# The output projection of a two-layer hybrid trunk computed as seven block products instead of eight

## The chip, the core and the metric

The kernel runs on one core of a Trainium2 chip. The metric is the device time of one execution in microseconds (us). All weights come from device memory during the execution, and all data is float32.

## What is computed

One trunk of two layers works on a sequence of 512 tokens, 1024 wide. What matters here is the middle of each layer:

```python
g_a, g_m = jnp.split(gates, 2, axis=-1)
mixed = jax.nn.sigmoid(g_a) * (att @ w_att_branch) + jax.nn.sigmoid(g_m) * (hm @ w_m_branch)
x = x + mixed @ w_out                       # 512x1024 @ 1024x1024

u = jax.nn.relu(rmsnorm(x, norm_ffn) @ w_ff1)   # 1024 -> 4096
x = x + (u * u) @ w_ff2                         # 4096 -> 1024
```

Ahead of it stand a normalisation, one large input projection, a windowed attention that gives `att`, and a matrix-memory branch that gives `hm` (both 512 wide). The text calls the second of them the m branch.

## The kernel before

**Precision by three products.** `mm3` (L182) makes every large product of three matmuls: each operand is cut into a high and a low part in a format that TensorE takes, and high x high, high x low and low x high are summed in PSUM. A cut takes one copy on ScalarE (the high part) and one subtraction on VectorE (the low part). Weights are cut by `chunk` (L139: one 128x512 tile at a time, copy L165, subtraction L166), activations by `split` (L171: L175 to L179). In the MLP `two_parts` (L866) cuts 128x1024 at a time (copy L867, subtraction L868).

**Groups of four banks.** Outside the MLP a projection is a list of steps from `group_steps` (L188): a group takes four PSUM banks (the pool `psum` holds five of them under the tag `m`, and `paux` three more), runs over the rows k of the weights with four 128-wide tiles m in the inner loop, and evacuates its four banks in `finish` once the last k is done. `feat_steps` (weights stationary, features on the partitions) and `tok_steps` (activations stationary, tokens on the partitions) build on it. `weave` (L222) places side work between the steps at positions counted in units of 12 matmuls.

**The end of the mixer** (L810 to L841) is the place of the change:

- Two groups for the m branch (L823 to L830), each with four k and four m, so 16 steps and 48 matmuls. `ev_m` multiplies the bank by the gate (L826), adds the attention branch's product (L827) and cuts the sum (`split`, L828).
- Two groups for the output projection (L834 to L840), each with eight k and four token blocks: 96 matmuls of 128x512. `ev_x` adds the four banks onto the residual stream `xtok` (L837). Four sets of four transposes for the next normalisation (`norm.steps`, L277) are woven into the second of them.

**The MLP** (L843 on) already uses seven block products in place of eight for its two matrix products: `first_slots` (L1008) and `second_slots` (L1167), with sums of weight blocks made by transfers that add to what lies in memory (`more`, L1025 and L1182, issued from GpSimd's queue) and with VectorE sums. There the products of the two matrices alternate, and each bank pair (`x`, `y`, `f`) rests for at least one product before it is used again. The first four loads of the MLP (`First.load`, L926) go to the buffers r0 to r3 of the pool `raws`.

**Who sets the order.** The kernel is written with Tile, a layer that gets the whole list of instructions with priorities, orders each engine's queue at compile time and places the waits; each engine then runs its queue strictly in order. `tc.high_priority()` puts what it encloses ahead of the rest. A buffer is given to a new tile once its old tile has been read for the last time, also across pools that share an address. SyncE (SP) issues the plain loads, GpSimd (POOL) the adding ones.

**Where pools lie.** The mixer holds, one after another, `wraw` 3 x 2 KB per partition, `wsp` 8 x 2 KB, `act` 32 x 2 KB, `tmp` 17 x 2 KB and `mid`. The MLP takes the same range over with `uraw`, `comb`, `uspl`, `spl` (8 x 4 KB) and `raws` (11 x 4 KB), in this order.

Of the kernel before, what the change touches and what calls it, by code (L numbers as in the profile page):

```python
# [16 lines left out]
P = 128  # L17
# [9 lines left out]
ROPE = 16  # L27
C_Q, C_K, C_V, C_QM, C_VM, C_OM, C_IF, C_G = 0, 512, 640, 768, 1280, 1792, 2304, 2312
NEG = -1.0e30
LN_EXP = "natural_log_exp_and_others"  # L30


@with_exitstack
def hybrid_kernel(ctx, tc, x, norm_mix, w_in, att_q_norm, att_k_norm, att_sinks, m_gate_bias,
# [27 lines left out]
    def nm(s):  # L62
        uid[0] += 1
        return f"{s}_{uid[0]}"
# [1 line left out]

    now = {}

    def pool(phase, name, bufs):
        now[name] = phase.enter_context(tc.tile_pool(name=name, bufs=bufs, reuse_waits="tile"))  # L70
# [137 lines left out]
    def feat_steps(acts, srcs, evac):  # L208

        def mm(ps, c, w, a, first, last):  # L210
            mm3(ps, w[0][:, c], w[1][:, c], a[0], a[1], first, last)

        return group_steps(acts, srcs, evac, T, mm)

    def tok_steps(acts, srcs, evac, width=T, order=None):

        def mm(ps, c, w, a, first, last):
            mm3(ps[:, :width], a[0][:, c], a[1][:, c], w[0][:, :width], w[1][:, :width], first, last)

        return group_steps(acts, srcs, evac, width, mm, order)  # L220

    def weave(fill, side=()):  # L222

        side = sorted(side, key=lambda e: e[0])
        at = 0.0
        for width, f in fill:
            while side and side[0][0] <= at + 1e-6:
                side.pop(0)[1]()
            f()
            at += width  # L230
        for _, f in side:
            f()

    def rsqrt(dst, v, tag):

        shape = list(v.shape)
        t = sm(shape, tag + "t")
        sc.activation(t, v, AF.Ln)
        sc.activation(dst, t, AF.Exp, scale=-0.5)
        t2 = sm(shape, tag + "u")  # L240
# [144 lines left out]
    nc.gpsimd.dma_start(grow[16:24, :], m_head_norm.rearrange("l (k p) -> (l k) p", p=P))  # L385
    wait_x.close()

    def mixer(l, norm, late, order, phase):

        W = w_in[l]  # L390
        pool(phase, "wraw", 3)
        pool(phase, "wsp", 4)
        pool(phase, "act", 32)
        pool(phase, "tmp", 17)
        mid = pool(phase, "mid", 1)

        def wcols(c0, n):
            return lambda k: [W[k * P:(k + 1) * P, c0:c0 + n]]
# [130 lines left out]
        def rope(xv, b, nh):  # L529

            r0 = 0 if nh == HQ else 8
            ct, st = tabs[nh != HQ]
            ve.tensor_tensor(xv, xv, rqk[:, b, r0:r0 + nh].unsqueeze(2).to_broadcast([P, nh, HD]), op=ALU.mult)
            t1 = sm([P, nh, ROPE], f"rp{nh}")
            t2 = sm([P, nh, ROPE], f"rq{nh}")
# [153 lines left out]
        def back(i):  # L689

            with tc.issue_after(i.ins):
                sc.preload_act_table_set(LN_EXP)

        def gate_steps(g, then=lambda: None):
            sg = []

            def ev(m, ps):
                sg.append(slot())
                ve.tensor_tensor(sg[m], ps, row[0], op=ALU.mult)  # L699
# [83 lines left out]
        prod = []  # L783

        def a_steps(g, sg):
            def ev_a(m, ps):
                t = sg[m]
                prod.append(t)
                ve.tensor_tensor(t, t, ps, op=ALU.mult)
# [22 lines left out]
        def head_tr(f):  # L812
            ps = aux()
            for b in range(NB):
# [6 lines left out]
        sgm = [g2, g3]  # L821
        mixed = [None] * KT
        for g in range(2):  # L823
            def ev_m(m, ps, g=g):
                i = 4 * g + m
                ve.tensor_tensor(sgm[g][m], sgm[g][m], ps, op=ALU.mult)  # L826
                ve.tensor_tensor(prod[i], prod[i], sgm[g][m], op=ALU.add)  # L827
                mixed[i] = split(prod[i])  # L828

            weave(feat_steps(hmT, lambda k, g=g: [w_m_branch[l, k * P:(k + 1) * P, 512 * g:512 * g + 512]], ev_m))  # L830


        norm = Norm(lambda k: g_ffn(l, k))
        for j in range(2):  # L834
            def ev_x(b, ps, j=j):
                xb = xtok[b // 2][j][:, b % 2, :]
                ve.tensor_tensor(xb, xb, ps, op=ALU.add)  # L837

            weave(tok_steps(mixed, lambda k, j=j: [w_out[l, k * P:(k + 1) * P, T * j:T * (j + 1)]], ev_x),
                  norm.steps(0, 1.5, 0.5) if j else [])  # L840
        return norm  # L841

    def mlp(l, norm, late, phase):  # L843
# [2 lines left out]


        final = l == DEPTH - 1
        quads = pool(phase, "uraw", 1)
        comb = pool(phase, "comb", 1)  # L850
        uspl = pool(phase, "uspl", 2)
        spl = pool(phase, "spl", 4)
        raws, idle_raws = pool(phase, "raws", 1), list(range(11))
        acts, ms = norm.acts, []
        H = 2 * P

# [405 lines left out]


        us = [{key: quads.tile([P, 4, H], F32, tag=t, name=nm("u")) for key, t in buf[0].items()}, {}, {}, {}]
        f01 = [First(0, "f"), First(1, "y")]
# [6 lines left out]
        slots = [first_slot(2, us[0], "x"), first_slot(3, us[0], "f")]  # L1272
        for part in range(4):
            p = second_slots(part, us[part])
            if part < 3:
# [34 lines left out]
    def turn_behind(norm, k):  # L1310

        with tc.issue_after(latest[0].ins):
            norm.turn(k)
# [4 lines left out]
            + [(3.0 + 2.2 * j, lambda j=j: norm.squares(j)) for j in range(2)])  # L1318
    order = None
    for l in range(DEPTH):  # L1320
        with start if l == 0 else ExitStack() as phase:
            if l > 0:
                psum_pools(phase, 3)
            norm = mixer(l, norm, late, order, phase)
        late = norm.steps(1, 1.5, 0.5)
        with ExitStack() as phase:
            psum_pools(phase, 2)
            norm = mlp(l, norm, late, phase)
        late = norm.steps(0, 1.5, 0.5, lambda k, norm=norm: turn_behind(norm, k)) if norm else []
        order = [4, 5, 6, 7, 0, 1, 2, 3]  # L1330

# [39 lines left out]
```

## Time and profile before

| What | Value |
|---|---|
| Time, median of 3 runs (lowest to highest) | 1303.55 us (1303.52 to 1304.15) |
| Span of the profiled execution, first to last instruction | 1302.9 us |
| The profiled execution's own time | not listed apart from these three; the median is 0.65 us above the span |
| TensorE matmuls / busy share of the span | 6978 / 99% |
| VectorE, ScalarE, GpSimd busy share | 73%, 59%, 15% |
| Output projection, layer 0 (first to last matmul) | 288.6 to 334.0 us |
| Output projection, layer 1 | from 933.8 us |

A span is what the trace covers. A busy share is an average over all stages. "Granted clock" is the share of its full clock that TensorE got; it is 1.00 for the whole execution. In the timeline, PE is TensorE's matmul queue, PEld its weight loads, DVE is VectorE, ACT is ScalarE; a row gives the start, the length of the run of like instructions, the engine, the line, output and inputs with shapes, and in brackets how long the engine had been idle and who ended that.

### The profile page before, as it was taken

Reading aid. Unit: us, or ns where it says so; the run is one execution under the profiler, and the core shown is the slowest. Engines: PE = TensorE matmul, PEld = TensorE weight load, DVE = VectorE, ACT = ScalarE, POOL = GpSimd, SP = SyncE. Lnnn points to the kernel's source line nnn. Section 1 sums busy time; section 2 is a strip of 40 time slices with the busy share of each in tenths; the row PEclk is TensorE's granted clock in tenths of the full one; section 3 lists DMA queues with packets and bytes.
Section 4 is the critical chain, followed back from the end, with each engine's and each line's share of the span. In section 5 each row is a group of like instructions: output and inputs, shape, how many; then the busy total and the mean of one; then the engine's idle time right before and its main releaser. Section 6 shows DMA issues by size and latency. Waiting matters only on the chain. (4 is left out here: it accounts for less than half of the span.)

```text
span 1302.9 us, 19074 instructions
## 1 busy us (share of the span) xinstructions
PE 1291.5 (99%) x6978; PEld 1105.2 (85%) x6978; DVE 955.5 (73%) x1505; ACT 763.7 (59%) x1329; POOL 200.4 (15%) x281
## 2 busy tenths in 40 slices
PE   9999999999999999999999999999999999999998
PEld 6877788888889999999888778888888899999987
DVE  4699754475677897968948996545737878879797
ACT  5578755544466665656555787554445556665563
POOL 4511100000003021131115111000000030311210
PEclk9999999999999999999999999999999999999999
DMA  5422222372369888898124222223714597988953
GB/s 154 110 72 59 74 81 74 90 249 82 98 155 172 236 185 207 195 211 216 33 75 114 65 66 75 79 75 92 256 57 129 141 215 195 201 212 196 213 148 98
DMA packets 130542, 177.61 MB, mean 136 GB/s; under 512 B 9864, under 2 KB 78320, under 8 KB 130448
## 3 DMA queue, kind: packets, MB, share of 16 engines
q1 hardware_dynamic: 94208, 131.82, 32.7%
q0 software_dynamic: 35520, 44.17, 21.2%
q8 instruction: 55, 0.90, 0.3%
q10 hardware_dynamic: 720, 0.40, 0.1%
q14 instruction: 39, 0.32, 0.1%
HBM read 174.27 MB, written 2.10 MB: 135 GB/s over the span
## 5 line engine op out<-in xcount | busy, mean ns | idle before, releaser
L47 PE MATMUL mm<-i,wh 128*128 128x512 f32 (+1 forms) x1280 | 352.7, 362 | 0.0
L867 ACT ACTIVATE wh<-raw 128x1024 fp32r<-128x1024 f32 x212 | 223.1, 1056 | 181.1 <-PE mm L47 114.0
L868 DVE TENSOR_TENSOR wl<-raw,wh 128x1024 fp32r<-128x1024 f32 x212 | 255.2, 1218 | 74.2 <-ACT wh L867 72.3
L47 PEld LDWEIGHTS mm<-i,wh 128*128 128x128 f32 x1280 | 224.3, 189 | 32.1 <-DVE a L699 0.8
L166 DVE TENSOR_TENSOR wl<-w,wh 128x512 fp32r<-128x512 f32 (+1 forms) x208 | 140.8, 679 | 137.7 <-ACT wh L165 129.4
L47 PE MATMUL mm<-i,wl 128*128 128x512 f32 (+1 forms) x640 | 229.8, 360 | 0.0
L165 ACT ACTIVATE wh<-w 128x512 fp32r<-128x512 f32 (+1 forms) x208 | 127.0, 611 | 146.7 <-PE mm L47 122.8
L47 PE MATMUL mm<-wh,uh 128*128 128x512 f32 x440 | 171.8, 390 | 0.0
L47 PE MATMUL mm<-wl,uh 128*128 128x512 f32 x440 | 171.7, 390 | 0.0
L47 PE MATMUL mm<-wh,ul 128*128 128x512 f32 x440 | 171.2, 389 | 0.0
L1027 POOL DMA_DIRECT2D raw<-in_w_ff_dram x48 | 62.3, 1304 | 591.3 <-DMA raw<-in_w_ff_dram 316.9
L47 PE MATMUL mm<-wh,i 128*128 128x512 f32 (+1 forms) x512 | 150.6, 370 | 1.2 <-ACT wh L165 0.6
L47 PEld LDWEIGHTS mm<-i,wl 128*128 128x128 f32 x640 | 120.8, 189 | 18.1 <-DVE wl L868 0.4
L47 PEld LDWEIGHTS mm<-wh,i 128*128 128x128 f32 x512 | 92.0, 188 | 19.0 <-DVE i L179 2.1
L913 DVE SCALAR_TENSOR_TENSOR x<-mm,ms,x 128x512 f32<-128x512 f32 x126 | 90.4, 743 | 9.9 <-PE mm L47 9.9
L47 PEld LDWEIGHTS mm<-wh,ul 128*128 128x128 f32 x440 | 82.6, 188 | 17.4
L47 PEld LDWEIGHTS mm<-wh,uh 128*128 128x128 f32 x440 | 82.8, 188 | 16.1
L47 PEld LDWEIGHTS mm<-wl,uh 128*128 128x128 f32 x440 | 82.8, 188 | 15.6
L47 PE MATMUL mm<-wl,i 128*128 128x512 f32 (+1 forms) x256 | 93.0, 363 | 0.0
L47 PE MATMUL mm<-wh,a 128*128 128x512 f32 x256 | 81.3, 392 | 0.0
L47 PE MATMUL mm<-a,wh 128*128 128x512 f32 x256 | 80.5, 397 | 0.0
L47 PE MATMUL aux<-i,wh 128*128 128x256 f32 x384 | 69.5, 283 | 0.0
(259 smaller groups left out, 2161.0 us busy)
## 6 DMA issues: line engine op xcount, KB each, us to landing
raw<-in_w_ff_dram SPq DMA_DIRECT2D x144, 512.0 KB, 5.2
raw<-in_w_ff_dram POOLq DMA_DIRECT2D x84, 512.0 KB, 7.8
w<-in_w_in_dram SPq DMA_DIRECT2D x128, 256.0 KB, 2.6
w<-in_w_out_dram SPq DMA_DIRECT2D x32, 256.0 KB, 2.7
w<-in_w_att_branch_dram SPq DMA_DIRECT2D x16, 256.0 KB, 2.6
w<-in_w_m_branch_dram SPq DMA_DIRECT2D x16, 256.0 KB, 2.7
w<-in_w_in_dram SPq DMA_DIRECT2D x16, 128.0 KB, 2.1
out_dram<-x SPq DMA_DIRECT2D x7, 256.0 KB, 2.0
```

What stands on the lines that cost most here:

```text
L47: latest[0] = nc.tensor.matmul(*args, **kw)
L165: sc.activation(wh[:, :off], raw[:, :off], AF.Copy)
L166: ve.tensor_tensor(wl[:, :off], raw[:, :off], f32(wh[:, :off]), op=ALU.subtract)
L867: sc.activation(hi, src, AF.Copy)
L868: ve.tensor_tensor(lo, src, f32(hi), op=ALU.subtract)
L913: ve.scalar_tensor_tensor(xh[:, cc], ps[i][:, cc], ms[j][:, b:b + 1], xh[:, cc], op0=ALU.mult, op1=ALU.add)
L1027: gp.dma_start(to[h], src(h, i, j), accum_op=ALU.add)
```

## The change

Four things are changed:

1. The two groups of the output projection become seven block products (24 matmuls each). `mixed` is taken as 2x2 blocks A(t,i), t a half of the tokens and i a half of the features, and `w_out` as 2x2 blocks B(i,j). The operands that are sums of A blocks (`s1` to `s4`) are made by VectorE and GpSimd (`combine`, `later`); the sums of B blocks by transfers that add one block onto another in memory (`more`).
2. The second half of the m branch runs with the tile m in the outer loop and k in the inner one, from two 128x1024 weight tiles that were cut ahead (`prep_m`), so that its four banks end one after another.
3. The PSUM pools of the MLP (three pairs `x`, `y`, `f` and two single banks) are opened ahead of the output projection and kept through the MLP.
4. In memory: the gated attention products move from eight `act` slots into two wide tiles (`prods`, 2 x 8 KB), `act` shrinks from 32 to 25 slots, `tmp` and `mid` move to the far end of the memory and are closed ahead of the output projection, where `wide_raw` (6 x 4 KB) and `wide_split` (8 x 4 KB) take their place; the MLP's `spl` and `raws` come first in its range. Four small tags get two buffers instead of three.

The core of the diff (the pools, the small tags and the attention products are left out):

```diff
+        parts_.close()
+        wide_raw, wide_split = pool(parts_, "wide_raw", 1, "right"), pool(parts_, "wide_split", 4, "right")
+        sgm, H = [g2, g3], 2 * P
...
+        def load(r, w, i, j, h):
+            with tc.high_priority():
+                nc.sync.dma_start(r, block(w, i, j, h))
+        def more(r, i, j, h):
+            with tc.high_priority():
+                gp.dma_start(r, block(w_out, i, j, h), accum_op=ALU.add)
...
+        def wide_parts(r):
+            with tc.high_priority():
+                h, lo = (wide_split.tile([P, 2, T], F32R, tag=t, name=nm(t)) for t in ("vh", "vl"))
+                sc.activation(h, r, AF.Copy)
+                ve.tensor_tensor(lo, r, f32(h), op=ALU.subtract)
+            return h, lo
+        def part(t, i, k):
+            return wide[i][:, 2 * k:2 * k + 2, H * t:H * (t + 1)]
+        def merge(g, m, ps):
+            ve.tensor_tensor(sgm[g][m], sgm[g][m], ps, op=ALU.mult)
+            ve.tensor_tensor(wide[g][:, m, :], wide[g][:, m, :], sgm[g][m], op=ALU.add)
...
+        weave(feat_steps(hmT, lambda k: [w_m_branch[l, k * P:(k + 1) * P, 0:T]], ev_m),
+              [(0.5, lambda: prep_m(0)), (1.0, lambda: prep_m(1))])
...
+        weights = {1: w1, 5: w5, 3: w3, 6: w6, 7: w7, 2: w2, 4: w4}
+        order = (1, 5, 3, 6, 7, 2, 4)
...
+        prepare(2)
+        for h in range(2):
+            with tc.high_priority():
+                u["00", h] = halves(part(0, 0, h))
+        def combine(k):
+            with tc.high_priority():
+                u1, u2, u4 = pair(), pair(), pair()
+                gp.tensor_tensor(u4, part(0, 0, k), part(0, 1, k), op=ALU.subtract)
+                ve.tensor_tensor(u1, part(1, 1, k), part(1, 0, k), op=ALU.subtract)
+                gp.tensor_tensor(u4, u4, u1, op=ALU.add)
+                u["s1", k] = halves(u1)
+                u["s4", k] = halves(u4)
+                ve.scalar_tensor_tensor(u2, u1, -1.0, part(0, 0, k), op0=ALU.mult, op1=ALU.subtract)
+                u["s2", k] = halves(u2)
+        for m in range(4):
+            ps = bank()
+            for k in range(4):
+                c = slice(m * P, (m + 1) * P)
+                hi, lo = wm[k // 2]
+                mm3(ps, hi[:, k % 2, c], lo[:, k % 2, c], hmT[k][0], hmT[k][1], k == 0, k == 3)
+            with tc.high_priority():
+                merge(1, m, ps)
+            if m % 2:
+                combine(m // 2)
+        small_banks.close()
+        psum_pools(wide_banks, 2)
+        def later(k):
+            u3 = pair()
+            gp.tensor_tensor(u3, part(0, 0, k), part(1, 0, k), op=ALU.subtract)
+            u["s3", k] = halves(u3)
+            for t in range(2):
+                u[f"{t}1", k] = halves(part(t, 1, k))
...
+        def onto(t, j, ps, op=ALU.add):
+            with tc.high_priority():
+                ve.tensor_tensor(xtok[t][j], xtok[t][j], ps, op=op)
+        plan = {1: ("x", "00", [(0, 1, ALU.add)]), 5: ("y", "s1", [(1, 0, ALU.subtract)]),
+                3: ("y", "s4", [(0, 0, ALU.subtract)]), 6: ("x", "s2", [(0, 0, ALU.subtract)]),
+                7: ("x", "s3", [(1, 0, ALU.subtract), (1, 1, ALU.add)]), 2: ("f", "01", [(0, 1, ALU.add)]),
+                4: ("y", "11", [(1, 1, ALU.add)])}
+        fresh = (1, 5, 2, 4)
...
+        weave([(0.125, lambda n=n, h=h, step=step: run(n, h, step))
+               for n in order for h in range(2) for step in range(4)],
+              norm.steps(0, 5.5, 0.25))
```

In `plan` the numbers are the names of the products; each has a bank pair, an operand and the quarters (t,j) of the residual stream onto which `onto` adds the pair when the product is done. A product has two halves h; each half takes one cut weight tile of 128x1024 (`prepare` cuts it three to four halves ahead, into one of four buffers) and runs four steps of three matmuls of 128x512. Products that are not in `fresh` add to what is in their pair: 3 goes on in `y` after 5, and 6 and 7 go on in `x` after 1. The additions in place are: onto the tile of product 1 the block for 5, then those for 6 and for 4; onto the tile of product 3 the block for 7. `later` runs behind product 1, without high priority.

More of the change, by code (lines that the diff above doesn't have):

```diff
@@ L386, in hybrid_kernel, with mixer @@
     wait_x.close()
-    def mixer(l, norm, late, order, phase):
+    def mixer(l, norm, late, order, phase, small_banks, wide_banks):
         W = w_in[l]
@@ L692, in back @@
                 sc.preload_act_table_set(LN_EXP)
+        wide = [prods.tile([P, 4, T], F32, tag=f"p{g}", name=nm("p")) for g in range(2)]
         def gate_steps(g, then=lambda: None):
@@ L697, in ev @@
             def ev(m, ps):
-                sg.append(slot())
+                sg.append(wide[g][:, m, :] if g < 2 else slot())
                 ve.tensor_tensor(sg[m], ps, row[0], op=ALU.mult)
@@ L833, in mixer @@
-        norm = Norm(lambda k: g_ffn(l, k))
[L834 to L840, printed above, removed]
+        parts_.close()
+        parts_ = ExitStack()
+        pool(parts_, "edge", 1, "right").tile([P, EDGE], F32, name=nm("edge"))
@@ new lines, in pair, with halves, ev_m, prep_m @@
+        def pair(dt=F32):
+            return slot(dt, (P, 2, H))
+        def halves(src):
+            return split(src, get=lambda: pair(F32R))
+        u = {}
+        def merge(g, m, ps):
+            ve.tensor_tensor(sgm[g][m], sgm[g][m], ps, op=ALU.mult)
+            ve.tensor_tensor(wide[g][:, m, :], wide[g][:, m, :], sgm[g][m], op=ALU.add)
+        def ev_m(m, ps):
+            merge(0, m, ps)
+        def prep_m(h):
+            r = raw(f"c{h}")
+            load(r, w_m_branch, 0, 1, h)
+            wm.append(wide_parts(r))
@@ new lines, in w6, with w7, w2, w4 @@
+        def w6(h):
+            return ra[h], lambda: more(ra[h], 1, 1, h)
+        def w7(h):
+            return rb[h], lambda: None
+        def w2(h):
+            rc[h] = raw(f"c{h}")
+            load(rc[h], w_out, 1, 1, h)
+            return rc[h], lambda: None
+        def w4(h):
+            return ra[h], lambda: None
+        weights = {1: w1, 5: w5, 3: w3, 6: w6, 7: w7, 2: w2, 4: w4}
+        order = (1, 5, 3, 6, 7, 2, 4)
+        preps, ready = [(n, h) for n in order for h in range(2)], {}
@@ new lines, in prepare @@
+        def prepare(n):
+            while preps and len(ready) < n:
+                key = preps.pop(0)
+                r, then = weights[key[0]](key[1])
+                ready[key] = wide_parts(r)
+                then()
+        prepare(2)
[12 more added lines that the diff above has]
+                u["s2", k] = halves(u2)
@@ new lines, in mixer, with run @@
+        fresh = (1, 5, 2, 4)
+        def run(n, h, step):
+            which, source, outs = plan[n]
+            if h == 0 and step == 0:
+                if n in fresh:
+                    now_in[which] = banks(which)
+                prepare(2 * order.index(n) + 4)
+            if h == 1 and step == 0:
+                prepare(2 * order.index(n) + 5)
+            hi, lo = ready[n, h]
+            ah, al = u[source, h]
+            k, i = step if isinstance(step, tuple) else (step // 2, step % 2)
+            c = slice(i * P, (i + 1) * P)
+            mm3(now_in[which][:, i, :], ah[:, k, c], al[:, k, c], hi[:, k, :], lo[:, k, :],
+                n in fresh and h == 0 and k == 0, False, skip_group_check=True)
+            if h == 1 and step == 3:
+                for t, j, op in outs:
+                    onto(t, j, now_in[which], op)
+                if n == 1:
+                    for kk in range(2):
+                        later(kk)
```

75 lines of the change are left out of this document (44 added, 31 removed).

## The prediction

> **What bounds the kernel now.** First the page: how full TensorE is, at which clock, and what the chain of waits says.
>
> ```profile
> span 1302.9 us, 19074 instructions
> ...
> PE 1291.5 (99%) x6978; PEld 1105.2 (85%) x6978; DVE 955.5 (73%) x1505; ACT 763.7 (59%) x1329; POOL 200.4 (15%) x281
> ...
> PEclk9999999999999999999999999999999999999999
> ...
> PE 41%; DVE 0%; ACT 0%; DVEq 0%; issue 0%
> ```
>
> Matmuls follow each other almost without a hole, at full clock, and no other engine ends a noticeable wait. So a matmul that goes is worth its whole slot, and any wait that the change puts into TensorE's queue costs its whole length. The windows show the same for the stage of the change (columns: stretch, length, then busy time and count of PE, PEld, DVE, ACT, POOL, granted clock, DMA share, GB/s): the m branch's last part, the output projection, and for comparison a stretch of the MLP, which already works by seven products.
>
> ```profile
> 270.00:275.00 5.00, 5.00 (x24) 4.14 (x23) 1.38 (x2) 1.28 (x3) 0.00 (x0) 1.00 1.01 347
> 277.00:289.00 12.00, 12.00 (x54) 9.70 (x53) 10.80 (x19) 4.20 (x9) 0.00 (x0) 1.00 0.95 319
> 289.00:334.00 45.00, 45.00 (x208) 37.23 (x207) 22.93 (x35) 19.85 (x34) 0.00 (x0) 1.00 0.21 65
> 575.00:635.00 60.00, 60.00 (x357) 53.55 (x356) 52.94 (x55) 37.39 (x38) 7.25 (x6) 1.00 0.74 181
> ```
>
> Two things are to be seen. The projection uses half of VectorE (22.93 of 45 us); and in the MLP VectorE is busy 52.94 of 60 us while TensorE misses nothing. VectorE at 88% is therefore harmless where the products alternate.
>
> The slot of a matmul comes from the timeline, from two like rows far apart in one unbroken run (36 triples lie between them):
>
> ```profile
> 289.09 0.61 PE L47 MATMUL mm<-wh,a 128*128 128x512 f32 x2
> ...
> 313.57 0.61 PE L47 MATMUL mm<-wh,a 128*128 128x512 f32 x2
> ```
>
> 24.48 us for 108 matmuls are **0.2267 us** each; the 0.39 us of a single row overlaps with its neighbours.
>
> **What goes.** Per layer 192 matmuls become 7 x 24 = 168: 24 x 0.2267 = **5.44 us** less. The transposes stay. The first seam of the m branch has a small wait that also goes, since its second half now frees its banks one by one:
>
> ```profile
> PEld mm L47 <- DVE a L826: 0.3, 1, 0.3
> ```
>
> That is 0.3 us. Together 5.74 us per layer.
>
> By the Trainium skill (TensorE: Matmul & The Clock Gate, Back-to-back issue gap) a sustained stream of 512-wide matmuls runs at about 131 ns each. By that, an estimate, the saving would be 24 x 0.131 = 3.1 us, and the sum below 2.3 us smaller per layer. The row above, 0.2267, decides.
>
> **What comes: waits for the bank pair.** Product 3 writes on in `y`, where product 5 has just ended, and `onto` must read the pair in between; 6 and 7 do the same in `x`. In the MLP no product follows on its own pair. The hand-over is put together from these rows: last matmul of a bank to VectorE, VectorE's end to TensorE, and the length of a PSUM addition of 128x1024.
>
> ```profile
> 275.29 0.39 PE L47 MATMUL mm<-a,wl 128*128 128x512 f32 x1
> 275.72 1.37 DVE L826 TENSOR_TENSOR a<-a,mm 128x512 f32<-128x512 f32 x2 [2.22 <-PE mm L47]
> ...
> 332.19 2.73 DVE L837 TENSOR_TENSOR x<-x,mm 128x512 f32<-128x512 f32 x4 [7.45 <-PE mm L47]
> ...
> 334.98 0.20 PEld L52 LDWEIGHTS aux<-ident,x 128*128 128x128 f32 x2 [0.26 <-DVE x L837]
> ```
>
> ```profile
> L1115 DVE TENSOR_TENSOR u<-u,mm 128x1024 f32<-128x1024 f32 x12 | 14.6, 1214 | 1.7 <-PE mm L47 1.7
> ```
>
> VectorE starts 0.43 us after the last matmul does, 0.20 after the next one could have; then 1.21; then 334.98 - 334.92 = 0.06. So 1.47 us if VectorE is free, up to one operation (1.2) more if not, 2.7. Queued behind the waiting matmul is everything TensorE has. But the order is made at compile time, and Tile fills such holes with later work: in these rows eight transposes, which the program puts three steps into the MLP, stand ahead of its first matmul.
>
> ```profile
> 334.04 1.38 PE L52 MATMUL aux<-ident,x 128*128 128x128 f32 x8
> 335.17 1.17 PE L47 MATMUL mm<-i,wh 128*128 128x512 f32 x4
> ```
>
> What could fill here is product 2: own pair `f`, weights that need no sum. Between 5 and 3 its operand is hardly cut (`later` has no priority): I take 1.6, between 0 and 2.7. Between 6 and 7 a buffer has become free and its first half can be cut: I take half, 0.8, same bounds.
>
> **What comes: VectorE's work, in front above all.** The prices, busy time from the groups by line, spacing in a run from the timeline:
>
> ```profile
> L867 ACT ACTIVATE wh<-raw 128x1024 fp32r<-128x1024 f32 x212 | 223.1, 1056 | 181.1 <-PE mm L47 114.0
> L868 DVE TENSOR_TENSOR wl<-raw,wh 128x1024 fp32r<-128x1024 f32 x212 | 255.2, 1218 | 74.2 <-ACT wh L867 72.3
> L826 DVE TENSOR_TENSOR a<-a,mm 128x512 f32<-128x512 f32 x16 | 10.7, 683 | 6.6 <-PE mm L47 6.6
> ```
>
> ```profile
> L505 POOL TENSOR_TENSOR t<-a 128x512 f32<-128x512 f32 x8 | 8.9, 1136 | 38.5 <-ACT a L407 38.5
> ```
>
> ```profile
> 265.21 2.48 DVE L699 TENSOR_TENSOR a<-mm,t 128x512 f32<-128x512 f32 x4
> ...
> 334.84 4.62 DVE L868 TENSOR_TENSOR wl<-raw,wh 128x1024 fp32r<-128x1024 f32 x4
> ```
>
> In a run a 512-wide operation takes (2.48 - 0.68) / 3 = 0.60 us, a 1024-wide one (4.62 - 1.22) / 3 = 1.13. Count from 275.7, when the first bank of the m branch's first half is done, to the end of product 1, at 277.6 + 10.9 + 5.4 = 293.9: 16 operations of `merge` 9.6 us, two low parts of operand 00 1.2, `combine` twice 6.1 (two sums and three low parts each), the first weight cut of product 5 1.1. That is 18.0 of 18.2 us. It fits only if the four wide cuts for the m branch's second half and product 1 (4.5 us) are done earlier, in the slack that 270:275 shows (VectorE busy 1.38 of 5), where the DMA is now full with MLP loads that can no longer come so early. So product 5 starts 0 to 4.5 us late; nearest is the row with the slack, and I take 0.5. Afterwards VectorE catches up: from 277.6 to the end (50.8 us) its sum is 44.8 us (merges 9.6, cuts of 12 halves 13.6, low parts and sums 10.9, seven of the eight `onto` 8.0, four transposed cuts 2.7), 88%, as in the MLP row. ScalarE's share is smaller in each item.
>
> **At nothing: the weight sums.** Each is a transfer of 512 KB added in place, like these of the MLP:
>
> ```profile
> L1184 POOL DMA_DIRECT2D raw<-in_w_ff_dram x36: 1189/1199/1409, 400.1 to 1271.7; - x36
> ...
> DMA to landing us min/median/max: 5.7/7.8/11.0
> ```
>
> The critical one is the second sum on product 1's tile: product 5's first cut ends about 16.7 us after the seam at 277.6, the sum lands at 24.6 (a `u3` on GpSimd, 1.1 us by the L505 row, may stand ahead of it: 25.7), two cuts (1.06 and 1.21) give 28, and product 6 starts at 16.3 + 0.5 + 10.9 + 1.6 = 29.3. It is hidden by products 5 and 3; at 11.0 instead of 7.8 it would cost about 2 us per layer. SP's loads stand in no one's way, its queue holds six of them in place of 16.
>
> **At nothing: the MLP's first weights.** Before, they are loaded from 265.7 on (the L929 row below). Now their buffers lie over tiles of the projection, the first over the second wide tile, the second over its end and the first `act` slot, both free long before product 2 unless an operand of product 4 sits there. If so, see below.
>
> **Sum.** Per layer -5.74 + 0.5 + 1.6 + 0.8 = -2.84; two layers -5.7. The span goes from 1302.9 to 1297.2; with the 0.65 us by which the median of the three runs stands above the span (no run is listed as the profiled one), **1297.9 us**.
>
> **The rivals.** No change is what lies within 0.2% (2.6 us), about what a measurement of this kernel can tell.
>
> - *All waits filled.* Product 2 fills both holes and product 5 is on time: 2 x 5.74 less, 1292.1. For it: the transposes in the rows above. Against: VectorE has 0.2 us to spare ahead of product 5. 0.17.
> - *The waits eat it.* Both holes stay (1.6 each) and product 5 is 2.5 late: 5.7 per layer, 1303.5. 0.08.
> - *VectorE's queue, the slow side.* At the seam into the products it still holds the wide cuts (4.5), and at both bank waits one more operation (2.7 each): 9.9 - 5.74 = 4.2 per layer, 1311.9. It decides from a stall of 5.74 + 1.3 per layer, 7.0, on. For it: 18.0 of 18.2 us, and 10.80 of 12 already now. Against: 88% over the stage. 0.20.
> - *Late weights for the MLP.* If the second buffer lies over an operand of product 4, its load starts as the projection ends: a landing (row below) of 6.5 plus two cuts, less 1.8 us of transposes, 6.9 per layer; 1297.9 + 13.8 = 1311.7. It decides from a load later than product 2. 0.08.
>
> ```profile
> L929 SPq DMA_DIRECT2D raw<-in_w_ff_dram x16: 379/460/787, 265.7 to 925.0; - x16
> ...
> DMA to landing us min/median/max: 4.6/6.5/8.5
> ```
>
> - *Starved transfers.* If VectorE's density delays what GpSimd issues, all sums land at 11.0: 2 us per layer, 1301.9. 0.05. The Trainium skill (SBUF — State Buffer, SBUF: two separate sides) says that a transfer issued from GpSimd can wait while VectorE holds a port that the two share. The rows speak against it: 1.19 to 1.41 us to issue one, beside a VectorE busy 52.94 of 60.
>
> **The numbers.** My forecast has 0.42 (its own range 1294.5 to 1300.9). With the first rival and a little of the fifth, faster has 0.62; within 0.2% 0.10; slower 0.28. For 8 in 10 the range is **1292.5 to 1309**: it leaves out the lowest part of the first rival and the dearest parts of the two slow ones.
>
> **What would show it.** Right: TensorE's projection stage shorter by about 5 us per layer; rows of `onto` ahead of product 3 with TensorE's weight load waiting for VectorE some 1.5 us. The step on VectorE is wrong if TensorE waits for a cut or an operand ahead of product 5 by more than 1 us; the one on transfers, if a cut waits for a DMA; the one on the MLP, if its first matmul waits. The whole is wrong if matmul slots differ from 0.2267 us.

## The result, and the profile after

The changed kernel takes **1354.22 us** (median of 4 runs, 1353.76 to 1355.12) against 1303.53 us of the kernel before on the same chip: a ratio of 1.0388, 95% interval 1.0373 to 1.0403. It is 50.7 us slower, 25 us per layer; forecast were 5.6 us less. All times below are medians beside runs of the kernel before on the same chip, which stood between 1303.5 and 1304.2 us.

The page of after, its first lines and the clock:

```profile
span 1352.2 us, 18992 instructions
...
PE 1302.6 (96%) x6930; PEld 1106.6 (82%) x6930; DVE 1004.7 (74%) x1517; ACT 781.4 (58%) x1333; POOL 238.9 (18%) x309
...
PEclk9999999999799999999999999999997999999999
```

48 matmuls are gone (6978 before), and yet TensorE has 50 us without work where before had 11, and in two slices its clock falls. The windows of the same stages as in the prediction, in the first layer (stretch, length, busy time and count of PE, PEld, DVE, ACT, POOL, clock, DMA share, GB/s); the products now end at 342.7, not at 334:

```profile
277.00:289.00 12.00, 12.00 (x53) 9.65 (x52) 11.64 (x17) 2.54 (x3) 2.52 (x2) 1.00 0.60 116
289.00:343.00 54.00, 45.93 (x188) 35.07 (x187) 44.87 (x43) 24.51 (x37) 15.79 (x12) 0.94 0.48 92
343.00:375.00 32.00, 22.02 (x85) 17.07 (x84) 20.47 (x27) 12.69 (x21) 1.30 (x1) 0.79 0.60 186
```

Two stages lose: in the products TensorE is idle for 8 of 54 us while VectorE has 44.87 us of work (before: 22.93 in 45), and at the start of the MLP it is idle for 10 of 32, at a mean clock of 0.79. The holes in the first half of the products, with what ended them:

```profile
292.32 0.49 PE L48 MATMUL mm<-vh,a 128*128 128x512 f32 x1 [0.35 <-ACT a L176]
294.94 1.07 PE L48 MATMUL mm<-vh,a 128*128 128x512 f32 x2 [1.89 <-DVE a L177]
305.56 0.79 PE L48 MATMUL mm<-vh,a 128*128 128x512 f32 x1 [3.69 <-ACT a L176]
310.65 0.73 PE L48 MATMUL mm<-vh,a 128*128 128x512 f32 x2 [0.69 <-DVE a L177]
```

All four end with the cut of an operand (lines 176 and 177), none with an addition onto `x`. At the start of the MLP it is a weight cut, and ahead of it SyncE's queue explains why (PE, ACT and SP rows of the timeline):

```profile
362.08 1.22 PE L48 MATMUL mm<-i,wh 128*128 128x512 f32 x2 [7.72 <-ACT wh L1021]
```

```profile
360.97 3.90 ACT L1021 ACTIVATE wh<-raw 128x1024 fp32r<-128x1024 f32 x4 [8.50 <-DMA raw<-in_w_ff_dram]
```

```profile
327.78 5.34 SPq L1083 DMA_DIRECT2D raw<-in_w_ff_dram  x3
342.67 6.74 SPq L1334 DMA_DIRECT2D raw<-in_w_ff_dram  x3
349.75 5.40 SPq L1083 DMA_DIRECT2D raw<-in_w_ff_dram  x5
```

Line 1083 loads the weights that the MLP needs first, line 1334 those of a product much later. Three loads of line 1083 go out at 327.78. Then three of line 1334 stand ahead of the rest; the first of them goes out at 342.67, when product 4 has ended, and the next five of line 1083 follow only from 349.75 on. The clock makes the holes dearer:

```profile
295.00:300.00 5.00, 5.00 (x15) 3.95 (x16) 4.78 (x5) 2.10 (x3) 4.04 (x3) 0.66 0.86 143
...
355.00:360.00 5.00, 0.00 (x0) 0.00 (x0) 0.00 (x0) 0.00 (x0) 0.00 (x0) 0.66 1.07 353
360.00:365.00 5.00, 2.88 (x6) 1.87 (x7) 2.94 (x3) 3.90 (x4) 0.00 (x0) 0.50 0.19 62
365.00:370.00 5.00, 5.00 (x19) 4.02 (x19) 4.93 (x5) 0.76 (x1) 0.00 (x0) 0.82 0.90 292
```

In the stretch 295 to 300 us TensorE is busy all the time and does 15 matmuls, behind a hole of 1.89 us. Before did 24 in the same five microseconds:

```profile
295.00:300.00 5.00, 5.00 (x24) 4.14 (x23) 2.67 (x4) 1.50 (x3) 0.00 (x0) 1.00 0.37 96
```

### The profile page after: what moved, and what is told of

The parts are those of the page before. It is cut to its first block, busy times and chain, and to the rows that moved or that the text cites. A ratio compares the mean times of both kernels' runs of the same rounds, so it can differ in the third digit from the quotient of the medians.

```text
span 1352.2 us, 18992 instructions
## 1 busy us (share of the span) xinstructions
PE 1302.6 (96%) x6930; PEld 1106.6 (82%) x6930; DVE 1004.7 (74%) x1517; ACT 781.4 (58%) x1333; POOL 238.9 (18%) x309
## 5 line engine op out<-in xcount | busy, mean ns | idle before, releaser
L48 PE MATMUL mm<-i,wh 128*128 128x512 f32 (+1 forms) x1280 | 357.4, 366 | 14.0 <-ACT wh L1021 14.0
L48 PEld LDWEIGHTS mm<-i,wh 128*128 128x128 f32 x1280 | 227.7, 192 | 46.9 <-ACT wh L1021 14.9
L48 PE MATMUL mm<-i,wl 128*128 128x512 f32 (+1 forms) x640 | 232.7, 364 | 0.1
L167 DVE TENSOR_TENSOR wl<-w,wh 128x512 fp32r<-128x512 f32 (+1 forms) x168 | 113.9, 679 | 106.1 <-ACT wh L166 97.8
L166 ACT ACTIVATE wh<-w 128x512 fp32r<-128x512 f32 (+1 forms) x168 | 102.0, 607 | 101.1 <-PE mm L48 86.1
L48 PE MATMUL mm<-vh,a 128*128 128x512 f32 x224 | 79.7, 426 | 14.1 <-ACT a L176 7.9
L48 PE MATMUL aux<-t,wh 128*128 128x256 f32 x384 | 69.5, 283 | 0.0
```

What stands on the lines that cost most here:

```text
L48: latest[0] = nc.tensor.matmul(*args, **kw)
L166: sc.activation(wh[:, :off], raw[:, :off], AF.Copy)
L167: ve.tensor_tensor(wl[:, :off], raw[:, :off], f32(wh[:, :off]), op=ALU.subtract)
```

## The experiments

Theories: **A**, VectorE's cuts are stretched by sums that run on GpSimd at the same time; **A'**, VectorE's work is what the products wait for; **C**, the MLP's first weights come late. Rivals: the bank-pair waits of the forecast, and weight sums that land late. Changes are made on after, or on the experiment named.

**1. The operand sums on VectorE (1347.01 us).** Also for lines 930 and 952:

```diff
-gp.tensor_tensor(u4, part(0, 0, k), part(0, 1, k), op=ALU.subtract)
+ve.tensor_tensor(u4, part(0, 0, k), part(0, 1, k), op=ALU.subtract)
```

> The six operand sums that each layer has on GpSimd (lines 928, 930, 952) are put on VectorE; the arithmetic is the same. Theory A (the port): the cuts and the sum of line 933 take up to twice as long only while a GpSimd sum runs; the trace of after has 8 cuts a<-a,a at 1.277 instead of 0.686 us, 15 weight cuts at 1.305 instead of 1.218, two L933 at 1.758, some 8.0 us of stretch per layer. With the sums on VectorE (6 x 0.68 = 4.1 us per layer) the cuts are back at 0.69 and 1.22 us and up to 3.9 us per layer go: about 1346 us, range 1343 to 1352. Theory B (VectorE is simply full, the port doesn't matter): its work grows by 4.1 us per layer and the time goes to about 1362 us.

VectorE's groups by form between 275 and 345 us (count, then busy time and mean ns of one), first after, then the experiment:

```profile
L849 DVE TENSOR_TENSOR vl<-wr,vh 128x1024 fp32r<-128x1024 f32 x15 | 19.4, 1305 | 3.2 <-ACT vh L848 3.2
L177 DVE TENSOR_TENSOR a<-a,a 128x512 fp32r<-128x512 f32 x8 | 10.1, 1277 | 1.4 <-ACT a L176 1.4
...
L933 DVE SCALAR_TENSOR_TENSOR a<-a,p 128x512 f32<-128x512 f32 x2 | 3.5, 1758 | 0.0
```

```profile
L849 DVE TENSOR_TENSOR vl<-wr,vh 128x1024 fp32r<-128x1024 f32 x15 | 18.2, 1222 | 5.3 <-ACT vh L848 5.3
...
L177 DVE TENSOR_TENSOR a<-a,a 128x512 fp32r<-128x512 f32 x8 | 5.5, 689 | 1.4 <-ACT a L176 1.4
```

The same cut takes 689 ns instead of 1277, and 7.2 us go although VectorE has six instructions more per layer. The accumulating transfers still go out from GpSimd's queue, so it is the sums and not these. A holds, B falls. The Trainium skill has this as a rule (SBUF — State Buffer, Who interferes with whom): a VectorE instruction with two inputs in SBUF contends with a GpSimd instruction that reads SBUF. By that, the trace agrees; how much it costs is the 1277 against 689.

**2. The weights early (1334.81 us).** The first four loads ahead in SyncE's queue, and their buffers over operands that are free by product 7:

```diff
+for n in idle_raws:
+    raws.tile([P, 4, H], F32, tag=f"r{n}", name=nm("raw"))
+idle_raws = [0, 7, 4, 5, 2, 6, 1, 10, 3, 9, 8]
...
+                    with behind():
+                        i = nc.sync.dma_start(r, w_ff1[l, ...
+                    if self.q < 2:
+                        lead[:] = [i]
```

`behind()` puts an instruction after the load in `lead`; line 1334 has it too.

> The MLP's raw weight buffers are placed so that the first four loads land over operands that are free by product 7, and these four loads come ahead of all other loads of the MLP in SyncE's queue; nothing else changes. Theory C (late weights): in each layer the 7.7 and 6.3 us that TensorE waits for the cut of line 1021, some 1.6 us of reduced clock behind each, and part of the 2.2 us of waits of the transposes go: about 17 to 20 us in all, 1334 to 1338 us. Rival (the weights only uncover the next wait, for the second half's transposes or the cuts on ScalarE): under 6 us, 1348 or more.

19.4 us, as theory C expected. **3. The order of the queue alone (1333.74 us)**, the same without moved buffers, that is, without the first three lines of the diff:

> after with one change: the MLP's first four weight loads stand ahead of all its other loads in SyncE's queue; no buffer is moved (the second one still lies over an operand of product 4's first half). In after this load is issued behind three loads of line 1334, the first of which waits for product 4's end (342.67 us), and lands at 361. Theory C1 (the queue's order): nearly all of the 19.4 us that weights_early won comes back, 1334 to 1338 us. Theory C2 (the place of the buffer, the rival of the prediction): the load still waits for product 4, 1345 us or more.

20.5 us: it was the queue. SyncE's rows show the first five loads of the MLP's weights (line 1089 here) out before the other line's first (1343):

```profile
328.49 12.99 SPq L1089 DMA_DIRECT2D raw<-in_w_ff_dram  x5
343.40 0.37 SPq L1343 DMA_DIRECT2D raw<-in_w_ff_dram  x1
```

Where the buffers lay cost nothing that this pair of runs can tell.

**4. Both mended (1325.98 us)**, the edits of 1 and 2 together.

> Both edits: the operand sums on VectorE and the MLP's first weights early. If the two costs lie one behind the other, their gains add: 1354 - 18 - 8 = 1328 us. What is then left over before, some 24 us or 12 per layer, is VectorE's work in the product stage. If they overlap: 1334 or more.

28.2 us go, a little more than 19.4 and 7.2 together. 22 us are left over before.

**5. Eight plain products (1323.62 us).** On 2, the projection as two row halves by four weight blocks:

```diff
-order = (1, 5, 3, 6, 7, 2, 4)
+weights = {1: w00, 2: w10, 3: w01, 4: w11}
+order = (1, 2, 3, 4)
...
+for t in range(2):
+    ah, al = u[f"{t}{i}", h]
```

> The m branch and the memory stay as after, with the MLP's weights early, but the projection is done as eight plain block products (two row halves by four weight blocks, each weight cut once and used for both row halves): no weight sums, no operand sums, 8 weight cuts in place of 14, 4 additions onto x in place of 9, and 24 more matmul pairs of operands per layer than in the seven products, 8 x 24 x 0.2267 us = 43.5 us per layer. Theory D (the seven products cost their VectorE work): the product stage runs at TensorE's rate and the time is that of before, 1300 to 1308 us. Rival E (the m branch's second half or the new memory layout costs too): 1315 us or more.

D falls in this form. Eight products without any sum are only 2.4 us faster than the seven of run 4, and 20 us slower than before: what is left is not the price of seven products alone, but also of the rest of the change, the m branch's second half and where its tiles lie.

**6. The right side moved by 32 bytes (1322.12 us)**, on 4:

```diff
-EDGE = 112
+EDGE = 104
```

> Both mended, and the spacer at the end of the right side is 104 floats instead of 112, so that all tiles of the right side start 32 bytes higher, at a multiple of 64 bytes instead of 32 beyond one. In after a triple of matmuls of the products takes 0.70 us, in before 0.68 (0.2333 against 0.2267 per matmul), at a granted clock of 1.00 in both. Theory G (the address of the moving operand): the slots go back to 0.68 per triple, 56 triples x 0.02 = 1.1 us per layer, up to 3 us with the m branch: 1323 us. Rival (something else about these operands or the load beside them): 1326 us, triples at 0.70.

Seven triples apart, in after and in the experiment, both at a clock of 1.00:

```profile
326.03 0.40 PE L48 MATMUL mm<-vl,a 128*128 128x512 f32 x1
...
330.93 0.40 PE L48 MATMUL mm<-vl,a 128*128 128x512 f32 x1
```

```profile
312.11 0.39 PE L48 MATMUL mm<-vl,a 128*128 128x512 f32 x1
...
316.87 0.39 PE L48 MATMUL mm<-vl,a 128*128 128x512 f32 x1
```

4.90 / 7 = 0.70 against 4.76 / 7 = 0.68 us: G holds for the products. But it is not a matter of the moving operand alone. In the m branch's second half the tiles that were moved (`vh`, `vl`) are the stationary operand, and the moving one (`a`, named first in a row) stays where it was. Nine triples apart there, again first in after:

```profile
282.01 0.63 PE L48 MATMUL mm<-a,vh 128*128 128x512 f32 x2
...
288.31 0.63 PE L48 MATMUL mm<-a,vh 128*128 128x512 f32 x2
```

```profile
282.43 0.62 PE L48 MATMUL mm<-a,vh 128*128 128x512 f32 x2
...
288.55 0.62 PE L48 MATMUL mm<-a,vh 128*128 128x512 f32 x2
```

6.30 / 9 = 0.70 against 6.12 / 9 = 0.68 us. Per layer that makes 56 + 16 triples of 0.02 us, 2.9 us in both layers. The time fell by 3.9 us; that the rest comes from the clock, which between 290 and 345 us stood at 0.97 in both_mended and at 1.00 here, is not shown.

**7. No operand sums (1311.08 us)**, on 4:

```diff
-u["s1", k] = halves(u1)
-u["s4", k] = halves(u4)
...
+u["s1", k] = u["s4", k] = u["s2", k] = u["00", k]
```

> Both mended, with a part of the computation left out: the sums s1, s2, s3 and s4 of operands are not formed and not cut; products 5, 3, 6 and 7 take product 1's operand in their place. VectorE loses 10 sums and 8 cuts per layer, 18 x 0.69 = 12.4 us, ScalarE 8 halves. Theory A' (VectorE's queue is what the products wait for): the product stage of both_mended has 5.4 us of idle TensorE and 1.7 us of reduced clock per layer, and these go: about 1312 us, and then the waits of products 3 and 7 for their bank pair, which the prediction put at 1.6 and 0.8 us per layer, come in sight: with them 1315 to 1317 us. Rival (the accumulating transfers of the weight sums come too late): the waits stay, 1324 us or more, now for the weight cuts.

290 to 325 us, first in both_mended, then here:

```profile
290.00:325.00 35.00, 29.59 (x110) 21.05 (x109) 29.50 (x37) 15.70 (x21) 7.24 (x6) 0.95 0.56 93
```

```profile
290.00:325.00 35.00, 33.92 (x149) 26.74 (x148) 25.68 (x27) 15.65 (x18) 7.24 (x6) 1.00 0.68 136
```

14.9 us. All that was taken away is VectorE's and ScalarE's work on operands, and TensorE's idle time in these 35 us falls from 5.4 to 1.1, with the same accumulating transfers and the same `onto`. A' holds, with one reserve: ScalarE's copies go too, and so does the chain of sum, copy and subtraction, so VectorE's share is not separated. ScalarE was busy for 15.70 of the 35 us, VectorE for 29.50. The bank-pair waits did not come in sight.

**8. No weight sums (1321.89 us)**, on 6, with line 839 left out:

```diff
-gp.dma_start(r, block(w_out, i, j, h), accum_op=ALU.add)
+pass
```

> aligned_right without the accumulating transfers: the weight sums are left out, so products 5, 3, 6, 7 and 4 multiply by a plain block; every cut and every operand sum stays. Theory A' (VectorE's work is what holds the stage) with H: the wait at the start of product 1 goes, as ScalarE no longer stands for a landing sum, but the waits for the operand cuts of lines 176 and 177 further on stay: 1316 to 1320 us. Rival (the sums come late all along the stage): all waits go, 1311 us or less, as in no_operand_sums less 3 us for the address.

No change against 1322.12, where 1316 to 1320 were expected. In the profiled executions two things cancel. TensorE's idle time falls from 32.1 to 29.1 us; the wait at the start of product 1 goes from 0.96 and 0.61 to 0.15 us. Its busy time grows from 1288.1 to 1291.8 us, for behind the next holes the clock now falls:

```profile
300.00:305.00 5.00, 3.54 (x9) 2.37 (x10) 4.62 (x7) 2.32 (x4) 0.00 (x0) 0.82 0.00 0
```

So the accumulating transfers are behind some 3 us of waits, and leaving them out did not shorten the kernel. ScalarE's wait ahead of product 5's weight cut, which the trace of aligned_right puts down to a transfer (8.15 us), stays here with 7.25 us and is then put down to TensorE, which still reads the cut buffers that the m branch uses. As the main cause the rival falls.

**9. Product 1's second operand first (1324.86 us)**, on 6: product 5's two weight cuts are put behind it on ScalarE and VectorE.

```diff
+        own = list(last_split)
...
+                with ExitStack() as behind:
+                    if key[0] == 5:
+                        for i in own:
+                            behind.enter_context(tc.issue_after(i.ins))
+                    ready[key] = wide_parts(r)
```

> aligned_right with one change of order: the cuts of product 1's second operand stand ahead of product 5's two weight cuts in ScalarE's and VectorE's queues. Theory H (a queue: in after ScalarE stands 7.9 and 1.6 us ahead of these weight cuts, which read a sum that is still landing, and the operand, complete at 286.2, is cut only at 291.65): the wait of 1.6 us at the start of product 1 (290 to 295 us of aligned_right has 3.43 of 5 us) goes, in both layers, and what stood behind it moves up: 1317 to 1320 us. Rival (product 5 then waits for its weights or its operand by as much): 1322 us.

2.7 us slower. The hole at product 1 went, and a longer one stands at product 5:

```profile
298.95 1.22 PE L48 MATMUL mm<-vh,a 128*128 128x512 f32 x2 [4.17 <-DVE a L177]
```

H falls: in this run the wait was only handed on. In the profiled executions TensorE's idle time hardly differs, 31.3 against 32.1 us in aligned_right, and its busy time grows by 2.3 us.

**10. The MLP's first buffers over the mixer's weight buffers (1323.02 us)**, on 4:

```diff
+front = pool(phase, "front", 1)
 spl = pool(phase, "spl", 4)
...
-r = raws.tile(list(shape), F32, tag=f"r{n}", name=nm("raw"))
+r = (front if n < 4 else raws).tile(list(shape), F32, tag=f"r{n}", name=nm("raw"))
```

> Both mended as in the last run, and in addition the MLP's first four weight buffers change places with its cut buffers: they lie over the mixer's own weight buffers, which no product uses, and at the start of the second layer the mixer's weight buffers lie over them in turn. Theory F (what is left at the two boundaries is a matter of where buffers lie): both_mended still shows 0.9 and 1.3 us of waits of the transposes at the start of each MLP, a stage at a reduced clock behind them, and 2.8 us for the cut of line 166 at the start of layer 2; with the weights cut before product 4 ends, matmuls stand between the transposes again. All together up to 12 us: 1314 to 1320 us. Rival (the transposes wait for the addition of product 4 whatever the weights do): only the start of layer 2 changes, 1321 us or more.

Only 3.0 us, the rival's number. The waits at the boundaries did go (for the weights of the second layer 0.6 us in place of 2.8), but the operand cuts of line 176 now cost 9.8 us instead of 4.3. The MLP's loads go out from 273.6 us on, not from 329.2, and ScalarE waits longer for product 5's sums:

```profile
291.65 1.06 ACT L848 ACTIVATE vh<-wr 128x1024 fp32r<-128x1024 f32 x1 [10.90 <-DMA wr<-in_w_out_dram]
294.17 1.06 ACT L848 ACTIVATE vh<-wr 128x1024 fp32r<-128x1024 f32 x1 [1.47 <-DMA wr<-in_w_out_dram]
295.14 0.61 ACT L176 ACTIVATE a<-p 128x512 fp32r<-128x512 f32 x1
```

That the sums land late because they share the engines with these loads is argued from this trace, not tried by itself. **11. With 6 and 9 added (1321.69 us):**

> front_buffers with the right side moved by 32 bytes and product 1's second operand cut first. front_buffers lost at the seam (9.8 us of waits for cuts of line 176 against 4.3 in both_mended) what it won at the boundaries. If theory H holds, that loss goes: 1323.0 - 3.9 for the address - 5.5 = 1313 to 1315 us. If the boundaries' gain was not there in the first place: 1319 us, as operand_first.

A miss; TensorE waits 4.9 us in one place for the next operand. **12. With 6 and 7 added (1311.10 us):**

> no_operand_sums (sums s1 to s4 left out, products 5, 3, 6, 7 take product 1's operand) with the address moved and the exchanged first buffers: what seven products would give if the operand sums cost VectorE nothing. By the earlier runs: 1311.1 - 3.9 for the address - 4 to 8 for the boundaries = 1299 to 1303 us. If it stays over 1304, something else than VectorE's sums also stands against the 24 matmuls saved per layer.

A miss too: behind ScalarE's wait for the sums stand holes of 4.3 and 5.0 us at product 1, with a clock of 0.60 after the first, and they take what the boundaries give. **13. and 14. Eight plain products with 6 and 10 (1311.05 us), and then with the cuts of product 1's operands earlier (1307.98 us):**

```diff
 u["00", h] = halves(part(0, 0, h))
+u["10", h] = halves(part(1, 0, h))
```

> The eight plain products with the exchanged first buffers of front_buffers and the right side moved by 32 bytes. If theory F holds for this kernel too, its boundary waits of some 2 x (2.2 + 1.7) + 4.5 us go, and if G holds 3 us more: 1323.6 - 12 - 3 = 1308 to 1312 us; what is then left over before is the seam at product 1, 1.3 us per layer, and the rest of the m branch's second half. Rival: 1318 us or more.

> eight_front with the cuts of the operand that product 1 needs for its second row half made as soon as their tiles are complete, before the m branch's second half, not behind it. eight_front waits 1.5 us per layer for such a cut: 1311 - 3 = 1308 us. Rival (VectorE is full there, and the weight cut or the additions of the m branch come late in its place): 1311 us.

Both came as expected: without sums the boundaries, the address and an operand's cut account for 15.6 of the 19.8 us by which run 5 was over before. Some 4 us are left; TensorE is then busy as long as in before (1291.3 against 1291.5 us) and idle for 14.9 us in place of 11.4, and no run shows why.

**15. Product 2 in second place**, on 6 (1322.47 us) and with 10 (1309.40 us):

```diff
-order = (1, 5, 3, 6, 7, 2, 4)
+order = (1, 2, 5, 3, 6, 7, 4)
...
+                u["01", k] = halves(part(0, 1, k))
```

> aligned_right with product 2, whose operand is cut without a sum, moved to second place (order 1, 2, 5, 3, 6, 7, 4), its operand cut ahead of the sums; all work is the same. Theory J (VectorE's work comes too early in the stage, not too much of it: in aligned_right VectorE is busy 44 of the 50 us from 280 to 330 and TensorE loses its 5.1 us in the stage before 320 us): 24 matmuls more stand between the m branch and the first operand that needs sums, 5.4 us, and most of the 2 x 5 us go: 1312 to 1315 us. Theory K (too much work in all): the waits move to later products: 1319 us or more.

> The same order of products with the exchanged first buffers of front_buffers. If J holds: the boundary waits (0.9 + 1.3 us and the start of layer 2, some 8 us in all) go as well: 1304 to 1308 us. If K: 1315 us or more.

By itself the new order gives nothing, K's number, because its gain is lost again at the MLP's start (2.3 us idle from 335 to 340, clock 0.83); with the buffers of run 10 it gives 13.6 us against front_buffers, where run 6 had 3.9 of these with the address. J's gain comes only under this condition: 1309.40 lies just above J's 1304 to 1308 and far below K's 1315.

**16. Sums in the order of need.** One instruction less for s4 (1305.88 us), and then s2 and s4 behind the operands of products 2 and 5 (1305.21 us):

```diff
-ve.tensor_tensor(u4, u4, u1, op=ALU.add)
+ve.scalar_tensor_tensor(u4, u2, -1.0, part(0, 1, k), op0=ALU.mult, op1=ALU.subtract)
...
+            if n == 2 and step == 0:
+                sums(h)
```

> front_plain_second with one sum less per half: s4 is formed as -s2 - a01 in one instruction in place of two, 2 x 0.69 us of VectorE per layer less, and s4 stands behind s2. If VectorE's early work is what is left of the waits (TensorE idle 1.3 us at 295 to 300 and 1.6 us at 305 to 310 us in each layer): up to 2.8 us in all, 1306 to 1309 us. Rival (the longer chain s1, s2, s4 puts the cut of s4 later than product 3 needs it): 1310 us or more.

> one_sum_less, and s2 and s4 with their cuts are formed behind the operands of products 2 and 5 of both halves instead of ahead of the second half's. The work is the same as in one_sum_less, in the order in which the products need it. If the order is what is left: most of the 2 x 4.2 us of idle TensorE between 290 and 345 us goes, 1301 to 1305 us. If it is the amount of work ahead of product 5: as one_sum_less.

The last has a ratio of 1.0008 to before (1.0000 to 1.0017): 49 us of the loss are gone, with seven products and all operand and weight sums. Between these two runs, which do the same work in another order, lie only 0.7 us, less than the spread of either (1305.65 to 1310.32 and 1304.19 to 1306.24): this pair does not tell the order from the amount. The products of the last, and a wait for a bank pair:

```profile
289.00:333.00 44.00, 42.52 (x191) 33.32 (x189) 39.27 (x48) 22.64 (x32) 7.24 (x6) 1.00 0.64 128
```

```profile
320.06 0.50 PE L48 MATMUL mm<-vh,a 128*128 128x512 f32 x1 [0.63 <-DVE x L967]
```

Why it is not faster than before shows in a mark in the MLP, the matmuls on `uh`, first in before, then here:

```profile
L47 PE MATMUL mm<-wh,uh x224: 389/389/473, 379.9 to 653.8; 128*128 128x512 f32 x112
```

```profile
L48 PE MATMUL mm<-wh,uh x224: 389/389/477, 380.1 to 654.0; 128*128 128x512 f32 x112
```

The products last from 289.58 to 332.66 us, 43.1 against 45.4 in before, so 2.3 of the 5.4 us arrive at their end. The other 3.1 are lost inside them, where the trace shows four short holes of 1.4 us in sum. The products also start 0.95 us later, and by the first matmul on `uh` the rest is lost to waits of the transposes and short holes at the MLP's start.

## Why the prediction was wrong, point by point

- **"At nothing: the MLP's first weights"** failed, and is the largest part that one edit gives back: 20.5 of 50.7 us. The rival *late weights* had the event at 0.08 and 6.9 us per layer, but for another reason, a buffer over an operand of product 4. Run 3 leaves the buffers where they were and wins as much as run 2: the order of the loads in SyncE's queue decides. The step looked at where four buffers lie and not at what else is queued ahead of them; "SP's loads stand in no one's way" counted the projection's loads alone.
- **"What comes: VectorE's work"** failed in size. It found 18.0 of 18.2 us, called 88% over the stage harmless as in the MLP, and took 0.5 us per layer. Run 7 gives 14.9 us in all, 7.5 per layer, at the undisturbed durations. The share over the stage was the wrong measure: in sums_in_turn the same products wait little with VectorE busy 39.27 of 44 us, 89%. That it is the order of its instructions, and how many of them are due right behind the seam, is borne out by run 15, where a product without sums in second place is worth some 10 us beyond the address, with run 10's buffers and only with them; the last pair of run 16 does not settle it. The rival *VectorE's queue* (0.20) had the mechanism, at 4.2 us per layer slower in sum.
- **A term was missing: GpSimd's sums stretch VectorE's cuts.** 7.2 us alone, 8.8 behind run 2. The prediction weighed the shared port for transfers only, and without these (run 8) the time stays the same.
- **The granted clock was left out.** Every hole was priced at its length. In after TensorE's idle time grew by 38.2 us (49.6 against 11.4), but its busy time is also 22.0 us above what 48 matmuls less would leave (1302.6 against 1291.5 - 10.9 = 1280.6); the address explains 2.9 of these. Behind the hole of 7.7 us, at 0.50, three matmuls take 365.21 - 363.93 = 1.28 us in place of 0.68:

```profile
363.93 1.05 PE L48 MATMUL mm<-i,wh 128*128 128x512 f32 x2
...
365.21 1.05 PE L48 MATMUL mm<-i,wh 128*128 128x512 f32 x2
```

The Trainium skill (TensorE: Matmul & The Clock Gate, Wait — 56ns, not 53.3ns?) gives 426.7 ns for a 512-wide matmul at the low clock; by that, the trace agrees: 1.28 / 3 = 0.427.

- **The slot.** "The whole is wrong if matmul slots differ from 0.2267": they did, 0.2333 in the products, from an address (run 6): 2.9 us by the slots, 3.9 by the time.
- **The bank-pair waits, 1.6 and 0.8,** did not occur in after. In the built order a product's matmuls stand in the holes, by bank pair (`x`, `y`, `f`) and number:

```
x 24 | y 12, x 8, y 2, x 1, y 10, x 4 | y 24 | x 11, f 7 | x 24 | f 17 | y 24
```

13 of product 6's matmuls stand ahead of product 3, four of them behind product 5's last; seven of product 2's stand ahead of product 7. The remark that Tile fills such holes was right, the terms should have been near zero. Where nothing else is late, one wait of 0.63 us is seen (run 16).
- **The seam of the m branch, -0.3,** turned round: product 1 waits 0.35 and 1.89 us for its second operand.
- **Right:** the 24 matmuls less per layer. The weight sums at nothing held for the time (run 8: 0.2 us), though some 3 us of waits hang on them.

The terms add up in this way, each measured on top of the one before: 19.4 for the MLP's loads, 8.8 for the port, 3.9 with the address, and 16.9 between aligned_right and sums_in_turn, for the order of VectorE's work, one sum and the places of the buffers: 49.0 of 50.7 us. Open is how much of the 16.9 belongs to each, since runs 10 and 15 help only together.

## What to carry to other kernels

Where a stage is lengthened by work on another engine, list that engine's instructions by the moment at which TensorE needs each, not by their sum over the stage; and list each in-order queue by what stands ahead of the first thing that the next stage needs. A saving of matmuls is worth its slots only while no operand comes late: here 10.9 us of slots drew some 60 us of waits, lower clock and longer slots, and all repairs together bought a draw. When a wait goes because its queue was rearranged, look one product further before counting the gain (run 9), and read idle time and busy time apart: a hole that goes can be paid for by a lower clock behind the next one (run 8).

## What the runs showed of the hardware

- With an operand's tiles moved by 32 bytes, by the kernel's layout from 32 beyond a multiple of 64 to such a multiple, a 512-wide matmul takes 0.2267 instead of 0.2333 us, at a clock of 1.00 in both; this is so where the tile is the moving operand and where it is the stationary one (run 6).
- Beside GpSimd's sums of operands, eight VectorE cuts of 128x512 took 1.277 us in the mean; without these sums 0.689 (run 1).
- The clock fell to 0.66 behind a hole of 1.89 us in after. The length of a hole alone does not tell: the same hole of 2.80 us at the start of the second layer is followed by a clock of 0.66 in after (680 to 685 us) and of 1.00 in aligned_right (665 to 670 us).
- The clock can differ between executions of one kernel: one_sum_less took 1305.65 us at a mean clock of 0.999 and 1310.32 at 0.995.
